# A hybrid decoder trunk on one Trainium2 core: the third and fourth attention steps move ahead of a value block and the convolution taps, and one small scale moves to GpSimd

## The chip, the cores and the metric

The kernel runs on one core of a Trainium2 chip. The metric is the device time of one execution in microseconds (us). The engines are named as in the profile: PE is TensorE's matmul side and PEld its weight loads, DVE is VectorE, ACT is ScalarE, POOL is GpSimd, SP is the queue that starts most of the DMAs.

## The reference

Two layers work on 512 tokens of width 1024 in float32. Each layer is a SwiGLU feed-forward part with half weight, a token mixer, and another feed-forward part with half weight. The change lies in the mixer:

```
h = rms_norm(x); a, g, q, k, v = split(h @ w_in)
conv_out = silu(rms_norm(causal_depthwise_conv31(a * sigmoid(g)) + conv_b))
# four heads, each with two maps (m = 0, 1) of 64 features; 128 value features a head
s[m] = q[m] @ k[m].T / 8 + bias[distance], masked to distance >= 0
a = softmax(s[0]) - lam * softmax(s[1])
diff_out = rms_norm(a @ v) * (1 - lam_init)
x = x + concat(conv_out, diff_out) @ w_out
```

## The kernel before

All matmuls with weights are made of three float32r products of high and low parts: ScalarE copies a weight chunk to its high part (`parts_of`, L100), and VectorE or GpSimd subtracts for the low part (L101). Chunks live in rings of tiles: five raw, four high, four low. A chunk's ring slots come free when its last matmul is done.

The program is written in one order, and a planner then orders each engine's instructions: an instruction is issued when its inputs and its tile's slot are there by the planner's own clock, and among those that are ready the one written earlier goes first. So an engine's queue is fixed when the kernel is built, but it is not the written order. Each queue is worked off in order on the chip.

The mixer goes through these stages. `conv_in` makes the four 128-channel tiles of the gated convolution input. `project` makes keys and queries with their norms; `to_features` transposes them. `project_values(j)` makes the values of token block j by 24 matmuls of 512 columns (L626 to L628) and a copy (L629); the values' weight chunks are loaded and split at its first call. `conv_taps(c, n)` runs the 31 taps of channel tile c: the first n on GpSimd (L663, L668) with products from ScalarE (L667), the others on VectorE in a PSUM bank (L675 to L680). `POOL_TAPS` is 31, 0, 0 and 10 for the four tiles.

Attention has 16 steps, `(i, h)`: token block i from the last to the first, and within it the four heads. `attend(n)` does parts of four steps, one behind the other:

- `softmaxes` of step n: two score matmuls (L714) into one bank of the PSUM tag `sc` and one of `po`, of (i + 1) x 128 columns; for each map the bias with the row minimum on VectorE (L718) and the exponential with its sum on ScalarE (L722); a reciprocal (L725); the second map's scale `c2` of 128 x 1 (L727); and the joined map `e0` (L728), the last reader of the `po` bank. Both tags have two banks.
- `keys_first` of step n - 2: transposes of the map (L735) and a copy (L737).
- `values` of step n - 3: matmuls with all value blocks up to i (L744), and for the last head the norm of the block: a square (L753), a sum (L755), a small addition and a power on GpSimd (L756, L214), a product (L759).
- `block_out` of a block five steps after its last head: transposes (L771) and the scaled copies into `acth` and `actl` (L773, L774).

`conv_finish` takes the row statistics of the convolution (L221, L225, L214 and a spread by L245 and L249), multiplies the four channel tiles by them on GpSimd (L694), and for each tile takes a tanh (L696), a product (L697), and the high and low parts (L698, L699). The output projection (`ps_out`, L163 to L167) then runs in three passes: the convolution half for all tokens, the attention half for the last 256 tokens, and the attention half for the first 256. Its tiles use the `sc` and `po` banks too. The `wout` chunks are split by L100 on ScalarE and L101 on GpSimd.

Of the kernel before, what the change touches and what calls it, by code (L numbers as in the profile page):

```python
# [15 lines left out]
ALU = mybir.AluOpType  # L16
# [7 lines left out]
NT = SEQ // P  # L24
# [43 lines left out]
def trunk(ctx: ExitStack, tc: tile.TileContext, xt, par, lamv, relb, onehot,  # L68
          gu1, dn1, wag, wqkv, wout, gu2, dn2, out):
    nc = tc.nc  # L70
    V, S, G, T = nc.vector, nc.scalar, nc.gpsimd, nc.tensor
# [14 lines left out]
    def bank(tag, name):  # L86
        return psum.tile([P, 512], F32, tag=tag, name=name, bufs=BANKS[tag])
# [15 lines left out]
    def chunk(src, eng=None):  # L103
        raw, hi, lo = ring("wraw"), ring("whi"), ring("wlo")
        nc.sync.dma_start(raw, src)
        parts_of(raw, hi, lo, eng)
        return hi, lo
# [83 lines left out]
    for k0, k1 in ((0, 1), (1, 4), (4, KT)):  # L191
        h = slice(k0 * P, k1 * P)
# [87 lines left out]
    def wpart(w, b, n=P):  # L280
        return w[0][:, b * n : (b + 1) * n], w[1][:, b * n : (b + 1) * n]
# [223 lines left out]
    nlam, gq, gsub, ghalf = [], [], [], []  # L505
# [35 lines left out]
    def mixer(l, pr, after):  # L541
        with tc.tile_pool(name="mix", bufs=1) as mp, tc.tile_pool(name="mt", bufs=2) as mt:
# [74 lines left out]
            def project_values(j):  # L617

                if 2 not in wts:
                    wts[2] = [chunk(wqkv[l, 2, kc], G) for kc in range(KT // 2)]  # L620
                t = slice(j * P, (j + 1) * P)
                ps = bank("mm", "ps_v")
                for k in range(KT):
                    wh, wl = wpart(wts[2][k // 2], k % 2, 512)
                    xh, xl = pr[k]
                    T.matmul(ps, xh[:, t], wh, start=k == 0, stop=False)  # L626
                    T.matmul(ps, xh[:, t], wl, start=False, stop=False)
                    T.matmul(ps, xl[:, t], wh, start=False, stop=k == KT - 1)  # L628
                S.activation(vv[:, j].rearrange("p h d -> p (h d)"), ps, AF.Copy, scale=row["c"][:, j : j + 1])  # L629
# [72 lines left out]
            steps = [(i, h) for i in reversed(range(NT)) for h in range(HEADS)]  # L702
            sums, pos, maps, ats = {}, {}, {}, {}

            def softmaxes(i, h):
                W = (i + 1) * P
                tq = slice(i * P, W)
                if h == 0:
                    sums[i] = small.tile([P, 2, HEADS], F32, tag="sums", name="sums")
                scs = [bank(tag, "ps_sc")[:, :W] for tag in ("sc", "po")]  # L710
                e0 = mt.tile([P, SEQ], F32, tag="e0", name="e", bufs=4)[:, :W]
                sm = sums[i]
                for m in range(2):
                    T.matmul(scs[m], qz[:, m, h, tq], kt[:, h, :W], start=True, stop=True)  # L714

                for m, (sc, e) in enumerate(zip(scs, (e0, scs[1]))):
                    mn = small.tile([P, 1], F32, tag=f"mn{m}", name="mn")
                    V.tensor_tensor_reduce(  # L718
                        out=e, in0=sc, in1=row["bias"][:, h, SEQ - W :], scale=1.0, scalar=3e38,
                        op0=ALU.add, op1=ALU.min, accum_out=mn,  # L720
                    )
                    S.activation(e, e, AF.Exp, bias=mn, scale=-1.0, accum_out=sm[:, m, h : h + 1])  # L722

                r2 = small.tile([P, 1], F32, tag="r2", name="r2")
                V.reciprocal(r2, sm[:, 1, h : h + 1])  # L725
                c2 = small.tile([P, 1], F32, tag="c2", name="c2")
                V.tensor_scalar(c2, r2, nlam[l], sm[:, 0, h : h + 1], op0=ALU.mult, op1=ALU.mult)  # L727
                V.scalar_tensor_tensor(e0, scs[1], c2, e0, op0=ALU.mult, op1=ALU.add)  # L728
                maps[i, h] = e0

            def keys_first(i, h):
                pt = bank("tp", "ps_at")
                for j in range(i + 1):
                    t = slice(j * P, (j + 1) * P)
                    T.transpose(pt[:, t], maps[i, h][:, t], ident)  # L735
                at = mt.tile([P, SEQ], F32, tag="at", name="at")
                S.activation(at[:, : (i + 1) * P], pt[:, : (i + 1) * P], AF.Copy)  # L737
                ats[i, h] = at

            def values(i, h):  # L740
                if h == 0:
                    pos[i] = bank("mm", "ps_o")
                for j in range(i + 1):
                    T.matmul(pos[i][:, h * VD : (h + 1) * VD], ats[i, h][:, j * P : (j + 1) * P], vv[:, j, h, :],  # L744
                             start=j == 0, stop=j == i)
                if h < HEADS - 1:
                    return
                po = pos[i]

                se = small.tile([P, HEADS], F32, tag="se", name="se")  # L750
                V.scalar_tensor_tensor(se, sums[i][:, 0, :], VD * EPS, sums[i][:, 0, :], op0=ALU.mult, op1=ALU.mult)
                sq = tmp.tile([P, SEQ], F32, tag="sq", name="sq")
                S.activation(sq, po, AF.Square)  # L753
                so = small.tile([P, HEADS], F32, tag="so", name="so")
                V.tensor_reduce(so, sq.rearrange("p (h d) -> p h d", h=HEADS), axis=AX.X, op=ALU.add)  # L755
                G.tensor_tensor(so, so, se, op=ALU.add)  # L756
                ro = rsqrt(so, HEADS)
                ov = mt.tile([P, HEADS, VD], F32, tag="ov", name="ov")
                V.tensor_tensor(  # L759
                    ov, po.rearrange("p (h d) -> p h d", h=HEADS),  # L760
                    ro.unsqueeze(2).broadcast_to([P, HEADS, VD]), op=ALU.mult,
                )
                outs[i] = ov
# [3 lines left out]
            def block_out(i):  # L767
                tq = slice(i * P, (i + 1) * P)
                po = pos[i]
                for h in range(HEADS):  # L770
                    T.transpose(po[:, h * P : (h + 1) * P], outs[i][:, h, :], ident)  # L771
                pt = po.rearrange("p (h t) -> p h t", h=HEADS)
                S.activation(ch[:, CT:, tq], pt, AF.Copy, scale=gsub[l])  # L773
                V.scalar_tensor_tensor(  # L774
                    cl[:, CT:, tq], pt, gsub[l], f32(ch[:, CT:, tq]), op0=ALU.mult, op1=ALU.subtract
                )

            def attend(n):
                if n < len(steps):
                    softmaxes(*steps[n])  # L780
                if 2 <= n < len(steps) + 2:
                    keys_first(*steps[n - 2])
                if 3 <= n < len(steps) + 3:
                    values(*steps[n - 3])
                if n >= 5 and steps[n - 5][1] == HEADS - 1:
                    block_out(steps[n - 5][0])
# [13 lines left out]
            nc.sync.dma_start(bias, skew[0])  # L800
            row["bias"] = bias

            for n in range(2):
                attend(n)
                project_values(NT - 1 - 2 * n)
                project_values(NT - 2 - 2 * n)
            for c in range(CT):
                conv_taps(c, POOL_TAPS[c])
            for n in range(2, len(steps) + 5):
                attend(n)  # L810
            conv_finish()

# [28 lines left out]
    for l in range(DEPTH):  # L841
        nxt = {}

        def then(l2, gain):
            def after(m):
                if m == 0:
                    nxt["p"] = Prep(l2, gain)
                nxt["p"].tile(m)
            return after

        def last(m):
            nc.sync.dma_start(out[m], x[:, m, :])

        ffn(pr, gu1[l], dn1[l], then(l, "mix_norm"), *((lead, aside) if l == 0 else ()))
        mixer(l, nxt["p"], then(l, "ffn2_norm"))
        ffn(nxt["p"], gu2[l], dn2[l], then(l + 1, "ffn1_norm") if l + 1 < DEPTH else last)
        pr = nxt["p"]
# [74 lines left out]
```

## Time and profile before

| | |
|---|---|
| median of 3 runs | 1796.04 us (1795.92 to 1796.19) |
| the profiled execution | 1796.31 us, span 1794.5 us |
| PE, DVE, ACT, POOL busy | 99%, 67%, 50%, 36% of the span |
| granted TensorE clock | 1.00 |

A profile is one execution; busy time is what an engine's records cover. Matmuls are pipelined and the ends in their records are modelled, so two neighbours overlap. In a timeline a row is the start, the duration, the engine, the line, the operation, `written tile <- read tiles`, shapes and a count; brackets hold the idle time of the engine ahead of it and what ended that. The mixer's attention lies at about 458 to 514 us in the first layer and 1349 to 1405 us in the second.

### The profile page before, as it was taken

How to read it: one execution, taken by the hardware profiler on the slowest of the kernel's cores; microseconds unless marked ns; L12 is line 12 of the kernel's file. 1: busy time of each engine (PE TensorE's matmuls, PEld its weight loads, DVE VectorE, ACT ScalarE, POOL GpSimd, SP SyncE). 2: the span in 40 equal slices, each digit the busy share in tenths (PEclk: the TensorE clock that was granted, in tenths of full speed). 3: DMA queues.
4: the chain of work that ended last, by engine and by line, in shares of the span. 5: the costliest groups of instructions: out<-in, count | busy, mean ns of one | idle time of the engine just before them, and what ended most of it. 6: DMA issues, size and time to landing. Idle time of an engine off the chain costs nothing.

```text
span 1794.5 us, 28356 instructions
## 1 busy us (share of the span) xinstructions
PE 1784.6 (99%) x10845; PEld 1590.1 (89%) x10845; DVE 1211.1 (67%) x1863; ACT 896.1 (50%) x1482; POOL 653.6 (36%) x460
## 2 busy tenths in 40 slices
PE   9999999999999999999999999999999999999999
PEld 7899899888788899899888998998887888998997
DVE  6976477568867867477576765765788587673762
ACT  6555265445744456256433643654558354552651
POOL 4242232269843132133102312412797331322420
PEclk9999999999999999999999999999999999999999
DMA  7466476323212366466333654663231133664651
GB/s 243 107 179 183 108 181 176 118 94 94 71 48 83 94 165 188 106 171 189 105 94 98 171 167 120 177 179 118 71 114 51 48 106 91 166 178 112 180 150 59
DMA packets 111721, 231.24 MB, mean 129 GB/s; under 512 B 12151, under 2 KB 33414, under 8 KB 111584
## 3 DMA queue, kind: packets, MB, share of 16 engines
q1 hardware_dynamic: 91488, 191.93, 33.4%
q0 software_dynamic: 19808, 37.33, 12.5%
q8 instruction: 85, 1.39, 0.3%
q14 instruction: 52, 0.43, 0.1%
q10 hardware_dynamic: 288, 0.16, 0.0%
HBM read 227.26 MB, written 3.42 MB: 129 GB/s over the span
## 4 chain that ended last, share of the span: by engine, by line
PE 96%; DVE 2%; issue 1%; ACT 1%; DMA 0%; SPq 0%; ACTq 0%; DVEq 0%
PE ps_pair L384 38%; PE ps_d L166 9%; PE ps_d L163 9%; PE ps_d L167 9%; PE ps_pair L167 5%; PE ps_pair L166 5%; PE ps_pair L163 5%; PE ps_pair L596 2%; PE ps_pair L597 2%; PE ps_pair L598 2%; PE ps_out L163 1%; PE ps_out L166 1%; PE ps_sc L714 1%; PE ps_out L167 1%; DVE actl L263 1%; PE ps_v L628 1%
## 5 line engine op out<-in xcount | busy, mean ns | idle before, releaser
L100 ACT ACTIVATE whi<-wraw 128x1024 fp32r<-128x1024 f32 (+2 forms) x599 | 465.9, 802 | 609.5 <-PE ps_pair L384 225.7
L101 DVE TENSOR_TENSOR wlo<-wraw,whi 128x512 fp32r<-128x512 f32 (+2 forms) x556 | 526.0, 968 | 212.6 <-ACT whi L100 208.4
L384 PE MATMUL ps_pair<-acth,wlo 128*128 128x256 f32 x1088 | 308.5, 284 | 0.0
L384 PE MATMUL ps_pair<-actl,whi 128*128 128x256 f32 x1088 | 308.5, 284 | 0.0
L384 PE MATMUL ps_pair<-acth,whi 128*128 128x256 f32 x1088 | 308.4, 283 | 0.0
L166 PE MATMUL ps_d<-hl,whi 128*128 128x512 f32 x704 | 274.2, 390 | 0.0
L167 PE MATMUL ps_d<-hh,wlo 128*128 128x512 f32 x704 | 273.4, 390 | 0.0
L163 PE MATMUL ps_d<-hh,whi 128*128 128x512 f32 x704 | 268.7, 390 | 0.0
L384 PE MATMUL ps_pair<-th,wlo 128*128 128x256 f32 x816 | 231.3, 283 | 0.0
L384 PE MATMUL ps_pair<-tl,whi 128*128 128x256 f32 x816 | 231.2, 283 | 0.0
L384 PE MATMUL ps_pair<-th,whi 128*128 128x256 f32 x816 | 231.2, 283 | 0.0
L146 POOL TENSOR_TENSOR wraw<-wraw 128x512 f32<-128x512 f32 x68 | 101.8, 1497 | 339.5 <-DMA wraw<-in_gu 272.2
L141 POOL DMA_DIRECT2D wraw<-in_gu x68 | 82.0, 1207 | 392.4 <-DMA wraw<-in_gu 228.6
L384 PEld LDWEIGHTS ps_pair<-acth,whi 128*128 128x128 f32 x1088 | 209.1, 192 | 0.3
L384 PEld LDWEIGHTS ps_pair<-actl,whi 128*128 128x128 f32 x1088 | 209.0, 192 | 0.3
L384 PEld LDWEIGHTS ps_pair<-acth,wlo 128*128 128x128 f32 x1088 | 209.1, 192 | 0.0
L480 DVE SCALAR_TENSOR_TENSOR x<-ps_d,x 128x512 f32<-128x512 f32 x96 | 64.7, 689 | 179.6 <-PE ps_d L167 179.3
L166 PE MATMUL ps_pair<-actl,whi 128*128 128x512 f32 x448 | 175.0, 391 | 0.3
L163 PE MATMUL ps_pair<-acth,whi 128*128 128x512 f32 x448 | 174.4, 394 | 0.5 <-ACT whi L100 0.3
L167 PE MATMUL ps_pair<-acth,wlo 128*128 128x512 f32 x448 | 174.5, 391 | 0.0
L384 PEld LDWEIGHTS ps_pair<-tl,whi 128*128 128x128 f32 x816 | 156.7, 192 | 0.7
L384 PEld LDWEIGHTS ps_pair<-th,whi 128*128 128x128 f32 x816 | 156.7, 192 | 0.6
(176 smaller groups left out, 3268.9 us busy)
## 6 DMA issues: line engine op xcount, KB each, us to landing
wraw<-in_gu SPq DMA_DIRECT2D x208, 256.0 KB, 4.0
wraw<-in_gu SPq DMA_DIRECT2D x104, 512.0 KB, 3.7
wraw<-in_gu POOLq DMA_DIRECT2D x68, 512.0 KB, 5.7
wraw<-in_wqkv SPq DMA_DIRECT2D x24, 512.0 KB, 3.7
wraw<-in_dn SPq DMA_DIRECT2D x84, 128.0 KB, 3.1
wraw<-in_dn SPq DMA_DIRECT2D x32, 256.0 KB, 3.1
wraw<-in_wag SPq DMA_DIRECT2D x16, 512.0 KB, 3.6
wraw<-in_wout SPq DMA_DIRECT2D x16, 512.0 KB, 3.6
```

The lines of the kernel that those rows point to most:

```text
L100: S.activation(hi, raw, AF.Copy)
L101: (eng or V).tensor_tensor(out=lo, in0=raw, in1=f32(hi), op=ALU.subtract)
L141: nc.gpsimd.dma_start(two.rearrange("p (b c) -> p b c", b=2), u[:, h[0]].unsqueeze(1).broadcast_to([P, 2, 512]), accum_op=ALU.add)
L146: G.tensor_tensor(more[:, h[0]], two[:, h[1]], whole[:, h[0]], op=ALU.add)
L163: first = T.matmul(ps, wh, xh, start=start, stop=False)
L166: T.matmul(ps, wh, xl, start=False, stop=False)
L167: T.matmul(ps, wl, xh, start=False, stop=stop)
L384: mm = T.matmul(ps, l, r, start=first and i == j == 0, stop=False, skip_group_check=True)
L480: V.scalar_tensor_tensor(x[:, m, :], ps, 0.5, x[:, m, :], op0=ALU.mult, op1=ALU.add)
L596: T.matmul(ps[n], xh[:, t], wh, start=k == 0, stop=False)
L597: T.matmul(ps[n], xh[:, t], wl, start=False, stop=False)
L598: T.matmul(ps[n], xl[:, t], wh, start=False, stop=k == KT - 1)
```

## The change

The scale L727 goes to GpSimd in the eight steps of token blocks 1 and 0 (256 and 128 columns), and stays on VectorE in the others. The written order of the start of attention changes: the third step's `attend(2)` is written between the last two value blocks, and `attend(3)` behind the last value block and ahead of the taps. Before, both stood behind the taps.

```
-                V.tensor_scalar(c2, r2, nlam[l], sm[:, 0, h : h + 1], op0=ALU.mult, op1=ALU.mult)
+                (G if i < 2 else V).tensor_scalar(c2, r2, nlam[l], sm[:, 0, h : h + 1], op0=ALU.mult, op1=ALU.mult)
...
-            for n in range(2):
-                attend(n)
-                project_values(NT - 1 - 2 * n)
-                project_values(NT - 2 - 2 * n)
+            attend(0)
+            project_values(3)
+            project_values(2)
+            attend(1)
+            project_values(1)
+            attend(2)
+            project_values(0)
+            attend(3)
             for c in range(CT):
                 conv_taps(c, POOL_TAPS[c])
-            for n in range(2, len(steps) + 5):
+            for n in range(4, len(steps) + 5):
                 attend(n)
             conv_finish()
```

## The prediction

> **What bounds the kernel now.** I read the page's busy shares and chain first, then the stages of the mixer by windows, then the waits inside the one stage with idle time, and last each engine's timeline there.
>
> ```profile
> span 1794.5 us, 28356 instructions
> PE 1784.6 (99%) x10845; PEld 1590.1 (89%) x10845; DVE 1211.1 (67%) x1863; ACT 896.1 (50%) x1482; POOL 653.6 (36%) x460
> PE 96%; DVE 2%; issue 1%; ACT 1%; DMA 0%; SPq 0%; ACTq 0%; DVEq 0%
> ```
>
> TensorE is 99% busy and makes 96% of the chain that ended last. The change adds no matmul and removes none, so it can gain only the time in which TensorE stands still: 1794.5 - 1784.6 = 9.9 us in all. The windows show what part of that lies around the edited lines. Columns: stretch, its length, then busy us (count) of PE, weight loads, DVE, ACT, POOL, the granted clock, DMA share, GB/s.
>
> ```profile
> 458.10:472.70 14.60, 14.60 (x58) 10.72 (x57) 12.04 (x26) 13.04 (x24) 13.27 (x11) 1.00 0.00 0
> 472.70:485.00 12.30, 12.30 (x64) 8.55 (x63) 8.79 (x30) 10.90 (x27) 12.05 (x8) 1.00 0.58 173
> 485.00:501.70 16.70, 14.76 (x97) 11.72 (x95) 15.95 (x61) 13.38 (x42) 9.01 (x9) 1.00 0.00 0
> 501.70:513.80 12.10, 11.82 (x62) 9.16 (x63) 12.10 (x36) 9.02 (x26) 2.93 (x5) 1.00 0.01 1
> 1375.90:1392.60 16.70, 14.73 (x98) 11.70 (x96) 15.95 (x61) 13.37 (x42) 9.01 (x9) 1.00 0.01 2
> 1392.60:1404.70 12.10, 11.85 (x62) 9.21 (x63) 12.08 (x36) 8.99 (x26) 2.90 (x5) 1.00 0.00 0
> ```
>
> In the first layer PE idles 16.70 - 14.76 = 1.94 us and then 12.10 - 11.82 = 0.28 us; in the second 1.97 and 0.25. That is 2.22 us a layer, 4.44 us in both. In the stretch from 485 DVE is the full engine (15.95 of 16.70, then 12.10 of 12.10). In the two stretches before, where PE never idles, DVE has room: 2.56 us of 14.60, then 3.51 of 12.30. So DVE rests while PE works through the value blocks, and PE rests later while DVE catches up. The timelines say so instance by instance; first PE, then DVE:
>
> ```profile
> 472.25 0.39 PE L627 MATMUL ps_v<-wlo,acth 128*128 128x512 f32 x1
> 472.48 0.39 PE L628 MATMUL ps_v<-whi,actl 128*128 128x512 f32 x1
> 472.70 1.88 PE L714 MATMUL ps_sc<-kt,qz 128*128 128x512 f32 x4
> 474.42 0.60 PE L735 MATMUL ps_at<-ident,e 128*128 128x128 f32 x4
> 501.73 0.51 PE L163 MATMUL ps_out<-acth,whi 128*128 128x512 f32 x1 [1.26 <-ACT acth L698]
> ```
> ```profile
> 465.25 0.74 DVE L728 SCALAR_TENSOR_TENSOR e<-ps_sc,c,e 128x512 f32<-128x512 f32 x1
> 468.12 3.12 DVE L680 SCALAR_TENSOR_TENSOR ps_y<-u,par,ps_y 128x512 f32<-128x512 f32 x4
> 473.76 0.69 DVE L718 CUSTOM_DVE_ANT_0 e<-ps_sc,bias 128x512 f32<-128x512 f32 x1 [2.52 <-PE ps_sc L714]
> 474.62 0.70 DVE L718 CUSTOM_DVE_ANT_0 ps_sc<-ps_sc,bias 128x512 f32<-128x512 f32 x1 [0.16 <-PE ps_sc L714]
> ```
>
> At 465.25 the first step frees its PSUM bank (L728 is the last reader). Yet the third step's scores start at 472.70, behind the last value matmul. DVE runs out of taps at 471.24 and stands 2.52 us until those scores arrive. The largest single PE idle, 1.26 us, comes at 501.73: the first output matmul waits for the convolution's first finished channel (`acth`, L698).
>
> **The change, part by part.** *Third step ahead of the last value block.* Value matmuls start 0.23 us apart (472.25 to 472.48), so a block of 24 takes 5.5 us. The third step's scores become free at about 466, which is while the next-to-last block runs. With the new order they go in front of the last block at about 472.7 - 5.5 = 467.2. The four score passes occupy 474.42 - 472.70 = 1.72 us, and the transposes behind them about 0.44 (0.60 by the record, with an overlapped end). So the last block ends about 2.2 us later, near 474.9, and the fourth step's scores follow it almost where they are now. PE loses nothing: the same instructions run in another order while PE is full. DVE's 2.52 us are filled: it takes the third step's two minima at about 468 and moves four taps into what was the gap. From 474 on DVE then has about 2.5 us less before it, and this is the lead with which it enters the full stretch from 485.
>
> *What the later value block moves.* It issues no DMA of its own, but its matmuls release the ring slots into which ScalarE splits the output weights. These are ACT's L100 and then POOL's L101:
>
> ```profile
> 468.82 1.06 ACT L100 ACTIVATE whi<-wraw 128x1024 fp32r<-128x1024 f32 x1
> 473.49 1.05 ACT L100 ACTIVATE whi<-wraw 128x1024 fp32r<-128x1024 f32 x1
> ```
> ```profile
> 469.96 2.41 POOL L101 TENSOR_TENSOR wlo<-wraw,whi 128x1024 fp32r<-128x1024 f32 x1 [0.19 <-ACT whi L100]
> 472.32 1.29 POOL L668 TENSOR_TENSOR yp<-yp,prod 128x512 f32<-128x512 f32 x1
> 479.45 2.38 POOL L101 TENSOR_TENSOR wlo<-wraw,whi 128x1024 fp32r<-128x1024 f32 x1
> 484.58 1.27 POOL L668 TENSOR_TENSOR yp<-yp,prod 128x512 f32<-128x512 f32 x1 [0.17 <-ACT prod L667]
> ```
>
> Four weight splits and five tap additions share POOL here with one pause of 0.19 us, and the last addition, 484.58 to 485.85, is what the convolution's statistics wait for. If the splits come 2.2 us later, the additions can take the room before them, and the convolution may be complete up to one split (2.4 us) sooner. Against this, the third step's exponentials now compete on ACT with the products that feed the additions. I take the sum of both at zero to -2.4 us and count no separate gain: the cap below already binds. The output weights themselves are covered: the last split ends at 481.83 and would end near 484, against a first use at 501.73. The DMA queue's next loads wait on such splits too (its longest wait of that kind from 400 to 560 us is 36.4 us), and most of them feed the feed-forward part after the mixer; 2 us there are hidden.
>
> ```profile
> SPq L105 <- POOL wlo L101: 129.1, 17, 36.4
> ```
>
> *Fourth step and the taps.* Four taps move behind two steps. DVE's own taps end at 471.24 and are not needed before the POOL additions end at 485.85, so a delay of 3 us has 14 us of cover.
>
> *The scale on GpSimd.* Per layer eight multiplies of 128x1 (L727, steps of 256 and 128 columns) leave DVE and enter POOL.
>
> ```profile
> L727 DVE TENSOR_SCALAR c<-r,nlam,sums 128x1 f32<-128x1 f32 x32 | 8.6, 269 | 0.2
> L531 POOL TENSOR_SCALAR gsub<-par 128x1 f32<-128x1 f32 x2 | 0.5, 241 | 0.2
> L535 POOL TENSOR_SCALAR ghalf<-par 128x4 f32<-128x4 f32 x2 | 1.3, 638 | 0.1
> ```
>
> DVE saves 8 x 0.27 = 2.2 us a layer, all in its full stretch. POOL pays between 8 x 0.24 = 1.9 and 8 x 0.64 = 5.1 us; I take 0.24, the row of the same shape, and POOL has 7.7 us free from 485 to 501.7 and 9.2 after it, so on a free POOL this costs nothing. Each multiply now sits between a DVE reciprocal and a DVE scale, so two hand-overs are added; while they run, DVE has other instructions queued. The Trainium skill speaks against the move: its page "GPSIMD Engine Reference", section "Performance versus the Vector engine", says that an elementwise operation passes two software dispatch hops and runs about twice as long as on VectorE. By that the multiply would be 0.54 us, an estimate, and POOL's sum 4.3 us; L531's 241 ns against 269 do not bear that out at this size.
>
> **The sum.** The lead of 2.5 us on DVE, and up to 2.2 us saved there, meet an idle time on PE of 2.22 us a layer. I let the lead remove the 1.94 and 1.97 us ahead of the first output matmul, and nothing of the 0.28 and 0.25 behind it, where PE waits on the chain tanh, multiply, copy of each channel. That is 3.9 us. The profiled execution took 1796.31 us, 1.8 beyond its span; the median is 1796.04. So the forecast is 1796.04 - 3.9 = 1792.1 us.
>
> **The rivals.** *The scale queues behind the four normalising multiplies (slower).* POOL takes its queue in order, and these rows show what that costs already; first DVE, then POOL:
>
> ```profile
> 497.71 0.68 DVE L755 TENSOR_REDUCE so<-sq 128x4 f32<-128x512 f32 x1
> 498.64 0.16 DVE L725 RECIPROCAL r<-sums 128x1 f32<-128x1 f32 x1
> 498.92 0.27 DVE L727 TENSOR_SCALAR c<-r,nlam,sums 128x1 f32<-128x1 f32 x1
> 499.22 0.49 DVE L728 SCALAR_TENSOR_TENSOR e<-ps_sc,c,e 128x256 f32<-128x256 f32 x1
> 499.62 1.29 DVE L697 SCALAR_TENSOR_TENSOR yp<-th,yp 128x512 f32<-128x512 f32 x1
> ```
> ```profile
> 497.00 1.27 POOL L694 TENSOR_TENSOR yp<-yp,rb 128x512 f32<-128x512 f32 x1 [3.82 <-ACT rb L249]
> 498.23 3.64 POOL L694 TENSOR_TENSOR u<-u,rb 128x512 f32<-128x512 f32 x3
> 501.83 0.20 POOL L756 TENSOR_TENSOR so<-so,se 128x4 f32<-128x4 f32 x1
> ```
>
> The small addition L756 was ready at 498.39, when L755 ended, and ran at 501.83, behind all four multiplies. A scale whose reciprocal ends at 498.80 would have the same place: 501.83 instead of 498.92, 2.9 us late. Queued behind it on DVE are L728 (499.22) and then L697 (499.62), the very instruction whose copy the first output matmul awaits; PE then has little else, since the step's transposes and its PSUM bank hang on L728 as well. At worst 2.9 us on each layer: 1796.04 + 5.8 = 1801.8 us. It decides where the planner puts a scale behind the four and L728 ahead of L697; with the lead of 3.9 subtracted in full, it ends at 1797.9. Against it: the planner orders by readiness, so the taken scale may stand between the multiplies (wait 1.2 us at most, paid by the lead), and DVE may have L697 in front. The page "Perfetto Trace Analysis" of the Trainium skill, section "Tensor Engine Instruction", calls GpSimd's queue strictly first in, first out; L756 agrees with it, 3.4 us late.
>
> *The lead does not reach PE (no change).* ACT is nearly full from 458 to 485 (13.04 of 14.60, 10.90 of 12.30) and POOL fuller (13.27 and 12.05). If products and exponentials only trade places, the convolution ends where it did, the first output matmul stays at 501.73, and PE's idle time only moves: 1796.0, between 1793 and 1799. The same comes out if the change does not do what it says: instructions are issued by readiness and not as written (L680's taps run at 468, although the source has them behind every value block), so the third step's scores may stay behind the last block.
>
> **How the numbers follow.** Forecast 0.46, the queue on POOL 0.31, no change 0.23. About 0.2%, 3.6 us, is what a measurement of this kernel can tell from no change. Of the forecast's case 0.04 stays within that, of the no-change case 0.22, and 0.01 goes beyond it on the slow side: faster 0.42, same 0.26, slower 0.32. The low end lets the convolution's earlier end and DVE's saving count as well, in slack that the modelled ends of PE hide: 2 x 2.2 = 4.4 us below the forecast, about 1788.0. The high end takes in the POOL case nearly whole: 1801.0. The forecast's own range is 1788.0 to 1794.0.
>
> **What would show it.** Right: in the PE timeline, four score passes and four transposes ahead of the last value block at about 467; no 2.5 us idle before L718 near 473; the first output matmul near 499 with less than 0.5 us idle before it; PE's idle from 485 to 502 below 0.5 us a layer. The scale: POOL rows of 0.24 us, with L728 within 0.5 us of its reciprocal's end. Wrong: DVE idle before L728 released by POOL, of 1 us or more, with a group L694 in front; then the rival holds. Wrong too: the last tap addition later than 486, or POOL rows of 0.5 us and more for 128x1.

## The result and the profile after

| | before | after |
|---|---|---|
| median of 6 runs | 1796.02 us (1795.92 to 1796.19) | 1805.9 us (1805.53 to 1806.16) |
| profiled execution, span | 1796.31, 1794.5 us | 1805.86, 1804.1 us |
| granted TensorE clock | 1.00 | 0.995 |

The changed kernel is slower by 9.9 us, ratio 1.0054 [1.0043, 1.0064]. The forecast was 1792.1 us, and the range ended at 1801.0. The mechanism is the first rival, the scale that queues on GpSimd; its price was 9.9 us where that rival had 5.8 at worst.

The page of after: span, busy times, chain.

```profile
span 1804.1 us, 28356 instructions
PE 1789.0 (99%) x10845; PEld 1595.5 (88%) x10845; DVE 1216.1 (67%) x1847; ACT 897.5 (50%) x1482; POOL 669.7 (37%) x476
PE 96%; DVE 2%; POOL 1%; issue 0%; DMA 0%; ACT 0%; SPq 0%; DVEq 0%
```

The shares hardly move; POOL enters the chain with 1%, where it had no entry. Two windows of after say where (columns as in the prediction):

```profile
485.00:501.70 16.70, 14.02 (x92) 11.29 (x91) 14.44 (x53) 13.07 (x40) 8.51 (x11) 1.00 0.05 19
501.70:513.80 12.10, 10.31 (x45) 8.15 (x46) 9.17 (x27) 7.61 (x22) 5.53 (x8) 0.72 0.01 2
```

PE idles 2.68 us (1.94 before) and then 1.79 us (0.28), DVE is no longer full behind 485 us, and the granted clock falls to 0.72. From the first score matmul to the last output matmul, by the starts in the PE timelines, the first layer's mixer takes 98.30 us where it took 94.64, and the second layer's 99.36 where it took 94.57: 8.45 of the 9.6 us of the spans. Another 0.64 and 0.62 us fall in the feed-forward parts behind them; I did not follow those.

The instances, in after. First PE at the moved step and at the stall; brackets hold the idle time and its releaser:

```profile
467.07 1.02 PE L714 MATMUL ps_sc<-kt,qz 128*128 128x512 f32 x2
471.15 1.02 PE L714 MATMUL ps_sc<-kt,qz 128*128 128x512 f32 x2
474.55 0.39 PE L628 MATMUL ps_v<-whi,actl 128*128 128x512 f32 x1
501.73 0.93 PE L771 MATMUL ps_o<-ident,ov 128*128 128x128 f32 x4 [2.06 <-DVE ov L759]
503.40 0.80 PE L714 MATMUL ps_sc<-kt,qz 128*128 128x128 f32 x2 [0.74 <-DVE e L728]
505.64 0.77 PE L163 MATMUL ps_out<-acth,whi 128*128 128x512 f32 x1 [1.02 <-DVE mn L718]
```

Then POOL at the stall, without a pause from 498.07 to 506.21:

```profile
498.07 0.20 POOL L756 TENSOR_TENSOR so<-so,se 128x4 f32<-128x4 f32 x1 [2.48 <-DVE so L755]
498.32 1.27 POOL L694 TENSOR_TENSOR yp<-yp,rb 128x512 f32<-128x512 f32 x1
499.55 1.02 POOL L214 TENSOR_TENSOR rs_y<-so,mhalf 128x4 f32<-128x4 f32 x1
500.53 1.49 POOL L694 TENSOR_TENSOR u<-u,rb 128x512 f32<-128x512 f32 x1
502.00 0.82 POOL L727 TENSOR_SCALAR c<-r,nlam,sums 128x1 f32<-128x1 f32 x1
502.78 2.58 POOL L694 TENSOR_TENSOR u<-u,rb 128x512 f32<-128x512 f32 x2
505.36 0.85 POOL L727 TENSOR_SCALAR c<-r,nlam,sums 128x1 f32<-128x1 f32 x1
```

And DVE, the reciprocals that feed the two scales and the joins that wait for them:

```profile
498.24 0.16 DVE L725 RECIPROCAL r<-sums 128x1 f32<-128x1 f32 x1
499.39 0.16 DVE L725 RECIPROCAL r<-sums 128x1 f32<-128x1 f32 x1 [0.79 <-ACT ps_sc L722]
502.86 0.48 DVE L728 SCALAR_TENSOR_TENSOR e<-ps_sc,c,e 128x256 f32<-128x256 f32 x1 [0.25 <-POOL c L727]
506.25 0.48 DVE L728 SCALAR_TENSOR_TENSOR e<-ps_sc,c,e 128x256 f32<-128x256 f32 x1
```

The third head's scale had its input at 498.40 and began at 502.00, 3.6 us later; the fourth's had it at 499.55 and began at 505.36, 5.8 us later. L728 is the last reader of the `po` bank, so the next scores that need that bank start only at 503.40, and the first output matmul at 505.64 (501.73 before). Before, the same chain from reciprocal to join took 0.6 us on DVE alone (498.64 to 499.22).

### The profile page after: what moved, and what is told of

Read it like the earlier page. It is cut to its first block, busy times and chain, and to the rows that moved or that the text cites. A ratio compares the mean times of both kernels' runs of the same rounds, so it can differ in the third digit from the quotient of the medians.

```text
span 1804.1 us, 28356 instructions
## 1 busy us (share of the span) xinstructions
PE 1789.0 (99%) x10845; PEld 1595.5 (88%) x10845; DVE 1216.1 (67%) x1847; ACT 897.5 (50%) x1482; POOL 669.7 (37%) x476
## 4 chain that ended last, share of the span: by engine, by line
PE 96%; DVE 2%; POOL 1%; issue 0%; DMA 0%; ACT 0%; SPq 0%; DVEq 0%
PE ps_pair L384 38%; PE ps_d L166 9%; PE ps_d L167 9%; PE ps_d L163 9%; PE ps_pair L166 5%; PE ps_pair L167 5%; PE ps_pair L163 5%; PE ps_pair L597 2%; PE ps_pair L596 2%; PE ps_pair L598 2%; PE ps_out L163 1%; PE ps_sc L714 1%; PE ps_out L166 1%; PE ps_out L167 1%; PE ps_v L628 1%; PE ps_v L627 1%
## 5 line engine op out<-in xcount | busy, mean ns | idle before, releaser
L146 POOL TENSOR_TENSOR wraw<-wraw 128x512 f32<-128x512 f32 x68 | 106.0, 1559 | 340.5 <-DMA wraw<-in_gu 225.4
```

Of the source, the lines that this page charges most:

```text
L146: G.tensor_tensor(more[:, h[0]], two[:, h[1]], whole[:, h[0]], op=ALU.add)
```

## The experiments

All times are medians; the kernel before, measured again beside them, took 1796.13 to 1796.18 us. "Mixer" is the first layer from its first score matmul to its last output matmul, as above.

**One half of the change alone.** e1 is the change with the scale on VectorE everywhere:

```
-                (G if i < 2 else V).tensor_scalar(c2, r2, nlam[l], ...)
+                V.tensor_scalar(c2, r2, nlam[l], ...)
```

> The new written order alone, all scales on VectorE. Queue theory (the loss comes from scales that wait on GpSimd behind the normalising multiplies): no loss is left, 1792 to 1797 us, and PE idles at most 2.2 us a layer between 485 and 514. Order theory (the moved steps themselves bring the attention and the convolution out of step): 1802 us or more, PE idle of 4 us a layer as in the changed kernel.

1796.02 us, ratio 1.0000 [0.9990, 1.0009]; mixer 94.54 us. The new order does nothing to the time. e2 is the kernel before with the scale on GpSimd for `i < 2`:

> The eight scales on GpSimd with the old written order. Queue theory: 1800 to 1806 us; in the GpSimd timeline a scale whose reciprocal ended at about 499 starts only behind all four normalising multiplies, 2.5 us late or more, and a VectorE wait released by GpSimd L727 stands before L728. Order theory: 1795 to 1798 us, since the scales alone cost nothing on a queue with free time.

1803.8 us, ratio 1.0042 [1.0027, 1.0057]. The loss sits in the scale, and the POOL timeline of e2 has the queue as the rival drew it:

```profile
497.81 3.20 POOL L694 TENSOR_TENSOR u<-u,rb 128x512 f32<-128x512 f32 x3
500.96 0.66 POOL L756 TENSOR_TENSOR so<-so,se 128x4 f32<-128x4 f32 x1
501.60 0.66 POOL L727 TENSOR_SCALAR c<-r,nlam,sums 128x1 f32<-128x1 f32 x2
```

**Which of the eight scales.** Three variants of one line, all in the order of the change:

```
e4:  (G if i < 1 else V)               # the four steps of 128 columns
e5:  (G if i == 1 and h > 1 else V)    # third and fourth head at 256 columns
e6:  (G if i == 1 and h < 2 else V)    # first and second head at 256 columns
```

> The changed kernel with only the four scales of 128 columns on GpSimd. Queue theory: the 256-column scales made the wait in front of the first output matmul, so most of the loss goes: 1794 to 1799 us. Order theory: 1804 us or more. If the price is a hand-over between engines for each scale, in any place, half the loss stays: about 1801 us.

> The changed kernel with only two scales a layer on GpSimd, those of the third and fourth head at 256 columns, which the planner puts behind all four normalising multiplies. Queue theory: these two carry the loss, 1801 to 1806 us, with 3 us or more between the end of the reciprocal and the scale. If each scale pays for a hand-over of its own, two of eight cost a quarter: about 1798.5 us.

> The changed kernel with only the first two heads' scales at 256 columns on GpSimd, which the planner puts ahead of the normalising multiplies. Queue theory: they find the queue free, 1795 to 1798 us. Hand-over theory: about 1798.5 us, the same as the other pair.

Against e1's 1796.02: e4 1796.6 (+0.6, ratio to before 1.0005 [0.9996, 1.0014]), e5 1803.42 (+7.4, 1.0043 [1.0028, 1.0058]), e6 1798.29 (+2.3, 1.0012 [1.0002, 1.0021]). They add up to 10.3, close to the whole 9.9. Two scales of eight a layer carry three quarters. They are the two that meet the normalising multiplies; PE, POOL, DVE of e5:

```profile
503.94 0.80 PE L714 MATMUL ps_sc<-kt,qz 128*128 128x128 f32 x2 [4.80 <-DVE e L728]
```
```profile
498.31 3.64 POOL L694 TENSOR_TENSOR u<-u,rb 128x512 f32<-128x512 f32 x3
501.92 0.68 POOL L756 TENSOR_TENSOR so<-so,se 128x4 f32<-128x4 f32 x1
502.59 1.09 POOL L727 TENSOR_SCALAR c<-r,nlam,sums 128x1 f32<-128x1 f32 x2
```
```profile
498.68 0.17 DVE L725 RECIPROCAL r<-sums 128x1 f32<-128x1 f32 x1 [0.42 <-ACT ps_sc L722]
503.40 0.88 DVE L728 SCALAR_TENSOR_TENSOR e<-ps_sc,c,e 128x256 f32<-128x256 f32 x2 [0.25 <-POOL c L727]
```

TensorE stands still 4.80 us in one piece. e4's four scales go through the same hand-over from DVE to POOL and back, after the multiplies (the longest wait in the first layer is 1.1 us), and cost no more than a measurement can tell.

e6 missed the 1795 to 1798 us of the queue theory and came out near the 1798.5 of the hand-over theory, which e4 speaks against. Its scales start within 0.2 us of their reciprocals. What differs from e1 is the planner's order on other queues. These rows are ACT of e6:

```profile
497.38 0.45 ACT L722 ACTIVATE ps_sc<-ps_sc,mn 128x256 f32<-128x256 f32 x1 [0.84 <-DVE se L751]
497.85 0.59 ACT L249 ACTIVATE rb<-ps_spread 128x512 f32<-128x512 f32 x1
```

The copy L249, which the multiplies need, now stands behind an exponential that itself waits; in e1 it stands ahead of it, at 496.77. So the four multiplies begin 40.38 us behind the first score matmul instead of 39.48, and the first output matmul 45.31 instead of 44.24. Two scales moved to GpSimd have reordered ScalarE's queue. Whether this is the whole loss of e6 was not tested. In after the multiplies begin at 40.38 us too.

**Queue or hand-over.** e3 takes the four multiplies off GpSimd, in the changed kernel:

```
-                    G.tensor_tensor(z, z, rcv, op=ALU.mult)
+                    V.tensor_tensor(z, z, rcv, op=ALU.mult)
```

> The changed kernel with the four normalising multiplies (L694) of each layer on VectorE, so that the scales find GpSimd free. Queue theory: no scale waits over 0.5 us and PE idles less than 2.5 us a layer; VectorE pays 4 x 0.7 = 2.8 us a layer in its full stretch, so 1796 to 1801 us. Order theory: 1805 us or more, as the order is unchanged and VectorE gets work on top.

1801.52 us, ratio 1.0031 [1.0019, 1.0043]: over the expected span, and not a clean cut. The multiplies now stood on VectorE (498.29 to 500.78) ahead of the join L728, which ran at 501.36; the wait had only changed its queue, and the two scales took 1.08 us each beside them. A cleaner cut leaves every engine its work and moves the multiplies in time: with fewer taps of the last channel tile on GpSimd, the convolution is complete sooner and they run before the scales' inputs are there. e13 is e5, and e14 the whole change, each with

```
-POOL_TAPS = (TAPS, 0, 0, 10)
+POOL_TAPS = (TAPS, 0, 0, 5)
```

> The kernel of e11 (written order of the change, 5 taps in place of 10, scale on VectorE; 1798.3 us) with the scale of the third and fourth head's 256-column step on GpSimd, as in e5. In e11 the four normalising multiplies on GpSimd end near 495.7 us instead of 501.9. Queue theory: the two scales, with their reciprocals near 497 to 498 us, now meet an empty GpSimd and wait for nothing; the 7 us that e5 lost against e1 fall to 1 us or less, 1797 to 1800 us. If the hand-over itself costs (two semaphores, a slower multiply, wherever the scale stands): the loss of 7 us stays, 1804 to 1806 us.

> The changed kernel whole, all eight scales on GpSimd, with 5 taps in place of 10. Queue theory: the scales no longer find the four multiplies ahead of them, and of the 9.9 us most goes: 1798 to 1801 us, the first two heads' 2 us (e6) possibly left. Hand-over theory: 1806 to 1809 us.

Their base is e11 below, the same taps with the scale on VectorE, 1798.34 us. Its ten times spread from 1796.77 to 1803.23 us and the traced execution is the shortest, so two comparisons are given. e13: 1800.81 us, 1.0027 [1.0016, 1.0038], above its expected 1797 to 1800; the two scales cost 2.5 us by the medians and not 7.4, and 4.3 us by the traced mixers of both layers and not 7.7. e14: 1799.14 us, 1.0018 [1.0008, 1.0028], as expected; all eight cost 0.8 us by the medians and not 9.9, and 2.0 by the mixers and not 8.6. The intervals of e13 and e14 overlap that of e11; neither reaches a loss like that of e5 or of after. POOL, DVE and PE of e14, then POOL of e13:

```profile
493.16 3.65 POOL L694 TENSOR_TENSOR u<-u,rb 128x512 f32<-128x512 f32 x3
496.80 1.18 POOL L727 TENSOR_SCALAR c<-r,nlam,sums 128x1 f32<-128x1 f32 x2
```
```profile
493.40 0.16 DVE L725 RECIPROCAL r<-sums 128x1 f32<-128x1 f32 x1 [0.35 <-ACT ps_sc L722]
```
```profile
498.21 0.70 PE L714 MATMUL ps_sc<-kt,qz 128*128 128x256 f32 x2 [1.80 <-DVE e L728]
```
```profile
492.69 3.20 POOL L694 TENSOR_TENSOR u<-u,rb 128x512 f32<-128x512 f32 x3
500.38 1.44 POOL L214 TENSOR_TENSOR rs_y<-so,mhalf 128x4 f32<-128x4 f32 x1
501.82 0.65 POOL L727 TENSOR_SCALAR c<-r,nlam,sums 128x1 f32<-128x1 f32 x2
```

In e14 the multiplies are over by 496.81, and the third and fourth heads' scales start 0.1 us behind their reciprocals. The first two heads' scales now meet the multiplies: the reciprocal of 493.40 is used only at 496.80, 3.2 us late, and PE stands 1.80 us for that join. In e13 the rest of the loss has a queue of its own: the reciprocal of 500.15 waits behind the power L214 until 501.82. So neither kernel has a free queue, and a wait of 3.2 us at the first head costs far less than the like at the third and fourth. The number of hand-overs is the same in e5 and e13, and in after and e14, and the loss is not: a fixed price of a hand-over is ruled out, and the place of the third and fourth heads' scales in GpSimd's queue is the cause of most of the loss. e13 and e14 also give VectorE five taps that GpSimd had, which shifts the attention in time; that was not separated from the queue.

**The clock behind the stall.** In after the granted clock is 0.50 from about 502 to 509 us, behind PE's idle time. How much of the loss is this? e7 is the changed kernel with 10 matmuls of 512 columns a layer behind the spread L245, whose result nothing reads; e9 is e5 with 20 of them (lines behind 692 are three further in both):

```
+                keep = bank("y", "ps_keep")
+                for n in range(20):
+                    T.matmul(keep, ones_r, ones_r.unsqueeze(1).broadcast_to([P, NT, P]), start=True, stop=True)
```

> The changed kernel with ten more matmuls a layer (512 columns, result unread) that the planner puts into PE's idle time ahead of the first output matmul; they take 2.3 us at the full clock. Clock theory (PE's idle stretch brings the granted clock down to 0.5 for about 7 us, and that is about 2 us a layer of the loss): the clock stays at 1.00 in this stage and the time falls to 1800 to 1803 us although PE does more. If the lower clock costs nothing, because PE waits in that stretch anyway: 1805 to 1808 us.

> The kernel of e5 (written order of the change, scale on GpSimd for the third and fourth head's 256-column step alone; 1803.4 us) with 20 matmuls of 512 columns per layer whose result nothing reads, placed in the 4.8 us that TensorE stood idle there. At the full clock they take 20 x 0.23 = 4.6 us. If the granted clock of 0.5 that follows the idle time carries a good part of the loss: the clock stays at 1.0 and some 2 us a layer come back, 1799 to 1801 us. If the wait alone carries it: 1803 to 1804 us, at a clock of 1.0.

e7: 1804.0 us, 1.0045 [1.0029, 1.0061]. The clock held in the first layer (1.00) and fell in the second (0.86 from 1392.6 to 1404.7), and the interval overlaps that of after, so the median settles nothing. Its four times do go with the clock of their execution, from 1802.55 us at 1.00 to 1805.65 us at 0.997. e9 is clearer. Windows of e5, then of e9, and PE of e9:

```profile
502.00:504.00 2.00, 0.06 (x1) 0.06 (x1) 1.75 (x4) 1.19 (x3) 2.00 (x4) 0.50 0.00 0
506.00:508.00 2.00, 2.00 (x11) 2.00 (x10) 1.96 (x11) 1.93 (x6) 0.00 (x0) 0.50 0.00 0
```
```profile
502.00:504.00 2.00, 2.00 (x13) 1.73 (x11) 1.21 (x3) 1.34 (x2) 2.00 (x3) 1.00 0.00 0
506.00:508.00 2.00, 1.75 (x12) 1.57 (x12) 2.00 (x10) 1.59 (x7) 0.00 (x0) 1.00 0.00 0
```
```profile
498.75 4.80 PE L693 MATMUL ps_keep<-ones_r 128*128 128x512 f32 x20
```

The twenty fill the idle time, the joins come no sooner (504.53 - 458.72 = 45.81 us behind the first score matmul, 503.40 - 457.64 = 45.76 in e5), and the clock stays at 1.00. e9 took 1801.88 us, 1.0028 [1.0017, 1.0038]. That lies between the two expectations. By the traces the mixers take 97.23 and 97.24 us, against 98.50 and 98.28 in e5 and 94.54 and 94.52 in e1: of e5's 3.9 us a layer the clock has 1.0 to 1.3, the wait itself the rest. By the medians it is 1.5 of 7.4 us, with overlapping intervals. So the clock is the smaller part; each traced figure comes from one execution.

**Why the new order brings nothing.** e8 is e1 with `conv_finish` written ahead of `attend(8)`. e10 and e11 are e1 with 7 and 5 in place of 10 in `POOL_TAPS`; e12 is the kernel before with 7.

> The new written order with all scales on VectorE, and conv_finish written ahead of the ninth attention step instead of behind the last, so that the convolution's statistics and its chain go first where both are ready. If the first output matmul is late because attention work passes the convolution on VectorE, it comes 1 us or more before 502 and the time is 1793 to 1795 us. If the chain is bound by its own latencies, nothing moves: 1795.5 to 1796.5 us.

> The written order of the change with the scale on VectorE (e1, 1796.0 us), and the number of taps whose products ScalarE makes and GpSimd adds for the last value block cut from 10 to 7, the other three going to VectorE. If the statistics of the convolution wait on GpSimd's last addition (485.4 us in e1, 2.65 us for two), they come up to 3 x 1.27 = 3.8 us sooner, the first output matmul up to 2 us a layer sooner, and the time is 1792 to 1795 us. If VectorE, now with 3 taps more (3 x 0.78 us), or the attention steps set that matmul: 1796 us within 1.

> As e10, with 5 taps in place of 10. If GpSimd's additions set the end of the convolution: 1792 to 1794 us, no better than e10 once VectorE's taps end later. If VectorE is the bound behind it: 1796 to 1799 us, above e10 by up to 2 x 0.78 us a layer.

> The kernel before with 7 taps in place of 10: what e10 does without the new order. If the lead that the new order gives VectorE matters once the convolution ends sooner, e10 is faster than this one by 1 us or more; if the order is worth nothing here too, both agree within 1 us.

e8: 1796.02 us, 0.9999 [0.9989, 1.0008]. e10: 1798.99, 1.0017 [1.0007, 1.0028]. e11: 1798.34, 1.0014 [1.0004, 1.0025]. e12: 1795.81, 0.9994 [0.9985, 1.0004]. e10 missed both of its ranges, and against e12 the new order loses 3.2 us where I had expected a gain or no difference; e11 lies in the 1796 to 1799 us given for VectorE as the bound, though not above e10 as that said. The times of e10 and e11 spread by over 6 us (1797.49 to 1804.9 and 1796.77 to 1803.23), the longer ones at granted clocks of 0.997 to 0.999, so their medians hold more than the taps and the order; their traces, at 1.00, took 1797.54 and 1796.77. In e8 the first L694 starts 39.48 us behind the first score matmul, as in e1: the other written place moved nothing, so e8 does not test an earlier convolution. In e12 the first multiply L694 starts at 493.22 us where it started at 497.00, so the convolution's chain is 3.8 us sooner, and its first finished channel (L698) ends at 497.92; yet the first output matmul is no sooner and the time is the same. POOL, PE, and windows of e12:

```profile
493.22 1.27 POOL L694 TENSOR_TENSOR yp<-yp,rb 128x512 f32<-128x512 f32 x1 [2.26 <-ACT rb L249]
```
```profile
498.87 0.70 PE L714 MATMUL ps_sc<-kt,qz 128*128 128x256 f32 x2 [0.92 <-DVE e L728]
502.43 0.48 PE L163 MATMUL ps_out<-acth,whi 128*128 128x512 f32 x1
```
```profile
485.00:501.70 16.70, 14.89 (x97) 12.06 (x95) 15.70 (x53) 12.69 (x38) 8.00 (x9) 1.00 0.01 1
501.70:513.80 12.10, 11.14 (x61) 9.16 (x61) 11.54 (x40) 8.34 (x26) 1.51 (x3) 1.00 0.00 0
```

PE idles 1.81 + 0.96 us there, more than the 2.22 us of before: its largest wait is now for a join of the narrow steps (0.92 us, L728). None of the fourteen kernels beats the one before by more than a measurement can tell.

## Why the prediction was wrong

*Two steps failed: the price of the scale, put at nothing, and the 3.9 us for the lead.* The forecast said that on a free POOL the scale costs nothing, because POOL has 7.7 us free from 485 to 501.7. The sum of free time was right; the wanted microseconds were not among it, since POOL is busy without pause just when the third and fourth heads' reciprocals end. In place of nothing, e2 shows 7.6 us for the scales alone and e5 7.4 us for two of the eight. I had the row that says so: L756, 3.4 us late in the profile of before. e1 shows the second step: the order alone gained 0.0 us where the sum had 3.9. The rival that I put below the forecast, at 0.31, is what happened.

*The size.* "At worst 2.9 us on each layer" was one scale's wait, with the multiplies running as before. Measured: two scales in sequence, 3.6 and 5.8 us, because a power and the first scale itself went between the multiplies, and the multiplies came later (498.32 instead of 497.00), behind the copy L249 that e6 shows moved. Against the rival stood that a scale taken between the multiplies waits 1.2 us at most: the third head's scale did stand between them and waited 3.6, behind two multiplies and the power L214. On PE the layers lose 3.66 and 4.79 us. e9 puts 1.0 to 1.3 us a layer of a like loss on the clock, a term the prediction did not have. The saved 2.2 us of DVE and the lead paid nothing back, though the rival counted on that in one of its two ends. The sign named for it, DVE idle of 1 us or more released by POOL, did not come: the row of 502.86 has 0.25 us, because DVE found other work; the wait shows on POOL and PE.

*The price of the scale itself.* I took 0.24 us, from L531. Measured in after: 0.34 us in most places, up to 0.85 beside VectorE operations with two inputs in SBUF. This answer on L727 gives minimum, median and maximum in ns for the seven that lie from 485 to 515 us:

```profile
L727 POOL TENSOR_SCALAR c<-r,nlam,sums x7: 341/342/849, 492.6 to 512.2; 128x1 f32<-128x1 f32 x7
```

The 0.54 us estimated from the page named there lies between these. It was not the cause: e4 pays it four times a layer for 0.6 us in all.

*The order: its parts came as said, its gain did not.* The third step's scores run at 467.07 (467.2 said), though its second map only at 471.15, in the middle of the last value block; the last value matmul is at 474.55 (474.9 said). The lead on DVE was 1.1 us and not 2.5: in the first two windows DVE is busy 12.93 + 8.99 us in e1 against 12.04 + 8.79. These rows of e1 show where the rest stayed, and its last two windows what PE made of it:

```profile
472.23 0.70 DVE L718 CUSTOM_DVE_ANT_0 ps_sc<-ps_sc,bias 128x512 f32<-128x512 f32 x1 [0.69 <-PE ps_sc L714]
474.66 0.17 DVE L725 RECIPROCAL r<-sums 128x1 f32<-128x1 f32 x1 [1.68 <-ACT ps_sc L722]
```
```profile
458.10:472.70 14.60, 14.60 (x57) 10.03 (x56) 12.93 (x28) 12.44 (x24) 13.44 (x11) 1.00 0.00 0
472.70:485.00 12.30, 12.30 (x65) 9.14 (x64) 8.99 (x27) 11.21 (x27) 12.22 (x8) 1.00 0.50 141
485.00:501.70 16.70, 16.09 (x106) 12.76 (x105) 16.23 (x63) 13.96 (x44) 8.16 (x9) 1.00 0.06 25
501.70:513.80 12.10, 11.46 (x56) 8.14 (x57) 10.51 (x33) 8.44 (x23) 4.01 (x5) 1.00 0.00 0
```

The gap of 2.52 us became waits of 0.69 and 1.68 us, the second for an exponential on ACT.

*The sum counted the wrong idle time.* PE's recorded idle time fell in e1 from 2.22 to 0.61 + 0.64 = 1.25 us, and the time did not move. The record's idle is no measure of what can be gained. Add up, over the stretch 457 to 552 us, by how much the distance from each matmul's start to the next exceeds the median of its line and shape in before (0.227 us for the value matmuls of 512 columns, 0.112 us for L744 at 128). Then before has 6.6 us of slack and e1 6.7: the idle time had only been spread into gaps that the modelled ends cover. Page "Perfetto Trace Analysis" of the Trainium skill, section "Identifying the Most-Contended Engine", warns that matmul busy share does not show how close a kernel is to its roofline, because pipelined matmuls look smaller in the trace. Here the share misleads the other way: a value matmul is recorded with 0.39 us and starts 0.23 us after the one before it, and the records hide about two thirds of the slack. What sets this slack is narrowed and not settled: it is not the end of the convolution (e12), and PE's waits in e1 are short, at most 0.33 us, and name several releasers (the copy L737, the join L728, the product L759).

*The second rival, no change,* was right for the order alone, and the wait of 1.68 us for ACT is of the kind that it named; how much of the missing gain is ACT's was not tested.

## What to carry to other kernels

Before a small operation on the path goes to a lightly loaded engine, look up what that engine's queue runs at the very microsecond when the operand is ready: the share of the whole stage says nothing, and a row that already waits there, like L756, shows the price. Where a planner orders the queues, look for what moved on the other engines too, like L249 on ScalarE. Then ask who waits for the operation, how many such waits follow one another, whether TensorE has other work meanwhile, and what a stall of TensorE does to its clock afterwards. Idle time in matmul records can vanish without any time being gained; the distance between starts shows it.

## What the runs showed of the hardware

- The same 128x1 multiply on GpSimd takes 0.34 us in most places and 0.76 to 0.89 us (1.08 us in e3) while VectorE runs operations with two inputs in SBUF (L241 in e6, L699 in after and e14, L694 in e3). Page "SBUF — State Buffer" of the Trainium skill, section "Who interferes with whom", names a port pair that VectorE and GpSimd share under an exclusive lock; the numbers agree.
- The granted clock fell to 0.50 behind idle times of TensorE well below 3 us. In e13 one idle piece of 1.82 us was followed by a clock of 0.50 until about 507 us:

```profile
502.60 0.66 PE L771 MATMUL ps_o<-ident,ov 128*128 128x128 f32 x4 [1.82 <-DVE ov L759]
```
```profile
504.00:505.00 1.00, 0.90 (x4) 0.69 (x4) 1.00 (x6) 0.63 (x2) 0.00 (x0) 0.50 0.00 0
506.00:507.00 1.00, 1.00 (x4) 0.74 (x3) 1.00 (x6) 1.00 (x6) 0.00 (x0) 0.55 0.00 0
```

  The 1.26 us of the kernel before and the 1.48 us of e11 had left it at 1.00. The length alone does not decide: in e7 the same two pieces, 1.0 and 1.5 us, left it at 1.00 in the first layer and were followed by 0.50 in the second, from 1401.0 to 1404.4 us. Page "TensorE: Matmul & The Clock Gate", section "What's actually happening", gives about 3.4 us of idle time for the fall and as much busy time for the return. The return agrees (some 3.4 us in e13), but in a stretch of sparse matmuls the fall came after a single idle piece of about half that length.
